# Stick-breaking attention: how densely the preparation of the latent attention is woven in

## The chip, the cores and the metric

The kernel runs on one core of a Trainium2 chip, as one program. The metric is the time of one execution on the device in microseconds (us), as the median of several. The core has five engines with a queue of instructions each: TensorE (PE, matrix products, with its weight loads as PEld), VectorE (DVE), ScalarE (ACT), GpSimd (POOL) and SyncE (SP, which here only starts transfers).

## The reference

Two transformer blocks over 512 tokens of width 1024. The first is a hybrid of pooling and forgetting attention. The second has two attentions side by side, a stick-breaking one and a latent one, and then a sparse feed-forward layer with 16384 experts (PEER). The change concerns the two attentions of the second block:

```python
h = rms_norm(x, attn_norm[l])
proj = h @ w_in[l]
sb_q, sb_k, sb_v, cq, ckv, k_pe = jnp.split(proj, IN_SPLITS, axis=-1)
sb = stick_breaking_attention(sb_q, sb_k, sb_v)          # 8 heads of 64
q = (rms_norm(cq, cq_norm[l]) @ w_uq[l])                 # 384 -> 8 heads of 96
kv = (rms_norm(ckv, ckv_norm[l]) @ w_ukv[l])             # 256 -> 8 heads of 64 + 64
...
q = rms_norm(q, q_norm[l]); k = rms_norm(k, k_norm[l])   # per head
# the last 32 of each head's 96 are rotated by position (rope)
mla = chunk_causal_softmax_attention(q, k, v)
x = x + concat(rms_norm(sb), rms_norm(mla)) @ w_o[l]
x = x + peer_ffn(rms_norm(x, ffn_norm[l]), ...)

# stick-breaking, by blocks of 128 queries, keys s < t:
z = q @ k.T * scale
log_fail = log_sigmoid(-z)
later = cumsum(log_fail, reverse=True) - log_fail
a = exp(log_sigmoid(z) + later); out = a @ v
```

## The kernel before

The program runs through the first block, the second block's attentions and the feed-forward layer one after the other. Products of weights with activations are made of three products of fp32r halves (`mm3`, lines 150 to 152: high by high, low by high, high by low); each weight is streamed in, and split into a high half by ScalarE (line 129) and a low half by a subtraction on the engine in `lo_eng` (line 130), which is DVE, and POOL during the first part of the preparation.

The stick-breaking attention (`sb_attention`) works in 24 steps of one or two pairs of head and query block. A step has at most 512 score columns: for each pair of heads there are two steps with blocks 0 and 2 (128 + 384 columns), two with block 1 (256) and two with block 3 (512). Over its life a step has scores and mask on TensorE (lines 1062, 1063), absolute value, exponential and logarithm on ScalarE, a maximum (line 1074), the running sum as a scan (line 1083) and a subtraction (line 1084) on DVE, a last exponential on ScalarE (line 1094), transposes on TensorE (line 1037), a copy of them by DVE or ScalarE in turn (line 1039) and the products with v (line 1044). The steps are overlapped in 27 rounds; each round gives up control three times, and such a place is a slot.

In these slots other work is drawn, a piece at a time, from a generator `fill2`. Its pieces are in this order: 12 halves of projection tiles for the queries and keys of the stick-breaking attention (`heads_qk`), and 64 pieces that prepare the latent attention (`prep`, line 854): 8 for the query latents, 4 transposes of them (line 197), 8 for the key latents, 4 transposes; then the query up-projection, norm, rotation and transposes of heads by tiles of 128 tokens, and the same for the keys. A query tile's norm is a chain over engines: squares on ScalarE (line 904), their sum and a scaling on DVE (lines 912, 165), a power on POOL (line 166), a multiplication on DVE (line 915), the rotation in six operations on POOL (lines 843 to 850), transposes on TensorE (line 955) and a copy (line 957). For a key tile the lines are 931, 940, 165, 166, 944 and 945, 955, 957; its products are copied at line 932. Key latents are normalised at line 883, also with a power of POOL. PSUM has two banks `mm` for the tiles of all these pieces.

The draw is by a rate: each slot adds the rate to a sum, and each full 1 draws a piece. When the stick-breaking attention has ended, the latent attention (`ml_attention`) starts; its first scores need piece 65, and what is still missing is drawn at once, one piece after the other. Its slots draw one piece each. What orders the instructions in the end is a scheduler that works when the kernel is built: it takes the pieces in the order of the program and may move an instruction ahead where it expects an engine to wait.

The two lines around the rates, and the loop that uses them:

```python
due += 1.0 if "row" in mixed else RATE2 if "sb_done" in mixed else RATE1
while due >= 1.0:
    next(fill)
    due -= 1.0
```

Of the kernel before, what the change touches and what calls it, by code (L numbers as in the profile page):

```python
# [60 lines left out]
def hybrid_mla_peer_kernel(ctx: ExitStack, tc: tile.TileContext, x, meta, gains, rows, bforget, wf, w1v, w1u, poolw,  # L61
# [680 lines left out]
    with ExitStack() as c2:  # L742
# [58 lines left out]

        ready = {0}
        mready = set()
        RATE1, RATE2 = 0.65, 1.0

        def heads_qk():

# [1045 lines left out]
```

## Time and profile before

| | |
|---|---|
| median of three runs | 2052.3 us (2051.57 to 2060.87) |
| profiled execution | 2054.51 us |
| its span, first to last instruction | 2052.6 us, 27008 instructions |
| TensorE busy | 1960.8 us (96%) |
| weight loads busy | 1675.8 us (82%) |
| DVE busy | 1372.1 us (67%) |
| ScalarE busy | 768.5 us (37%) |
| POOL busy | 531.9 us (26%) |
| mean granted clock of TensorE | 0.982 |

The busy time of an engine is the time in which it had an instruction under way; TensorE's ends are modelled, so a busy TensorE is not one at its peak. The shares are means over stages with different limits: the feed-forward layer fills the second half of the span, and the stage of the change lies between 478 and 720 us. In the views below a group or a row has the line, the engine, the operation, and the tiles as out<-in; "idle before <-releaser" is the time that the engine stood before it, and what it then waited for.

### The profile page before, as it was taken

How to read it: one execution, taken by the hardware profiler on the slowest of the kernel's cores; microseconds unless marked ns; L12 is line 12 of the kernel's file. 1: busy time of each engine (PE TensorE's matmuls, PEld its weight loads, DVE VectorE, ACT ScalarE, POOL GpSimd, SP SyncE). 2: the span in 40 equal slices, each digit the busy share in tenths (PEclk: the TensorE clock that was granted, in tenths of full speed). 3: DMA queues.
4: the chain of work that ended last, by engine and by line, in shares of the span. 5: the costliest groups of instructions: out<-in, count | busy, mean ns of one | idle time of the engine just before them, and what ended most of it. 6: DMA issues, size and time to landing. Idle time of an engine off the chain costs nothing.

```text
span 2052.6 us, 27008 instructions
## 1 busy us (share of the span) xinstructions
PE 1960.8 (96%) x10297; PEld 1675.8 (82%) x10297; DVE 1372.1 (67%) x2574; ACT 768.5 (37%) x1228; POOL 531.9 (26%) x476
## 2 busy tenths in 40 slices
PE   7999999999998989998899999999999999999999
PEld 5777688877876778988889788888888888888887
DVE  4324423564577559998997677777777777777785
ACT  4323323254665332223554333333333333333332
POOL 1001100100165026654000133333333333333331
PEclk9999999999999999999999999999999999999999
DMA  4211132422112042213888788888988888888885
GB/s 161 82 62 42 42 102 84 137 77 72 47 42 78 27 154 100 86 52 128 250 244 279 262 295 307 307 282 300 309 292 307 286 297 311 288 308 291 305 279 179
DMA packets 138129, 387.63 MB, mean 189 GB/s; under 512 B 10624, under 2 KB 59904, under 8 KB 129808
## 3 DMA queue, kind: packets, MB, share of 16 engines
q1 hardware_dynamic: 48576, 216.65, 29.6%
q0 software_dynamic: 36864, 134.23, 19.9%
q10 hardware_dynamic: 52560, 35.03, 5.8%
q8 instruction: 80, 1.31, 0.3%
q14 instruction: 49, 0.40, 0.1%
HBM read 357.04 MB, written 28.84 MB: 188 GB/s over the span
## 4 chain that ended last, share of the span: by engine, by line
PE 62%; DVE 16%; issue 8%; DMA 7%; POOL 3%; ACT 3%; ACTq 0%; DVEq 0%; SPq 0%; POOLq 0%
PE mm L152 9%; PE mm L150 9%; PE mm L151 9%; DMA gat<-in_peer_u,idx 4%; PE s L151 3%; PE s L152 3%; PE s L150 3%; PE pt L151 3%; PE pt L152 3%; PE pt L150 3%; DMA gat<-in_peer_v,idx 3%; POOL gat L1616 2%; PE av L1044 1%; PE s L561 1%; PE mi L150 1%
## 5 line engine op out<-in xcount | busy, mean ns | idle before, releaser
L1616 POOL DMA_INDIRECT gat<-in_peer_u,idx x128 | 147.2, 1150 | 466.5 <-DVE acc L1634 233.2
L1616 POOL DMA_INDIRECT gat<-in_peer_v,idx x128 | 147.8, 1154 | 292.7 <-DVE pre L1630 185.3
L1390 DVE TENSOR_TENSOR vlo<-xt,vhi 128x1024 fp32r<-128x1024 f32 x94 | 115.0, 1224 | 126.9 <-ACT vhi L1389 126.1
L152 PE MATMUL mm<-h_hi,ulo 128*128 128x384 f32 x568 | 192.2, 338 | 8.0 <-DVE ulo L1390 8.0
L1389 ACT ACTIVATE vhi<-xt 128x1024 fp32r<-128x1024 f32 x94 | 99.6, 1060 | 262.9 <-PE mi L152 213.0
L150 PE MATMUL mm<-h_hi,uhi 128*128 128x384 f32 x568 | 193.5, 341 | 1.8 <-ACT uhi L1389 1.8
L151 PE MATMUL mm<-h_lo,uhi 128*128 128x384 f32 x568 | 191.3, 337 | 0.0
L130 DVE TENSOR_TENSOR wlo<-wraw,whi 128x2048 fp32r<-128x2048 f32 (+1 forms) x42 | 96.1, 2289 | 136.1 <-ACT whi L129 136.0
L1634 DVE SCALAR_TENSOR_TENSOR acc<-gat,pre,acc 128x1024 f32<-128x1024 f32 x128 | 164.0, 1281 | 33.5 <-DMA gat<-in_peer_v,idx 33.2
L1630 DVE CUSTOM_DVE_ANT_0 gat<-gat,xt 128x1024 f32<-128x1024 f32 x128 | 155.9, 1220 | 42.1 <-DMA gat<-in_peer_u,idx 42.0
L152 PE MATMUL mm<-h_hi,h_lo 128*128 128x384 f32 x456 | 157.3, 345 | 14.8 <-DVE h_lo L1390 10.8
L150 PE MATMUL mm<-h_hi 128*128 128x384 f32 x456 | 157.8, 346 | 10.3 <-ACT h_hi L1389 10.3
L151 PE MATMUL mm<-h_lo,h_hi 128*128 128x384 f32 x456 | 155.9, 342 | 0.0
L129 ACT ACTIVATE whi<-wraw 128x2048 fp32r<-128x2048 f32 (+2 forms) x53 | 97.5, 1840 | 111.0 <-PE mm L151 59.0
L152 PEld LDWEIGHTS mm<-h_hi,ulo 128*128 128x128 f32 x568 | 107.3, 189 | 10.2 <-DVE ulo L1390 10.2
L150 PEld LDWEIGHTS mm<-h_hi,uhi 128*128 128x128 f32 x568 | 107.8, 190 | 4.5 <-ACT uhi L1389 2.7
L151 PEld LDWEIGHTS mm<-h_lo,uhi 128*128 128x128 f32 x568 | 107.6, 189 | 1.8
L150 PE MATMUL mm<-hT_hi,whi 128*128 128x512 f32 x256 | 104.7, 409 | 1.3 <-DVE fz L417 1.0
L150 PE MATMUL s<-vhi,w_hi 128*128 128x512 f32 x256 | 100.3, 392 | 5.0 <-ACT w_hi L1710 5.0
L152 PEld LDWEIGHTS mm<-h_hi,h_lo 128*128 128x128 f32 x456 | 88.0, 193 | 19.4 <-DVE h_lo L1390 14.5
L151 PE MATMUL mm<-hT_lo,whi 128*128 128x512 f32 x256 | 102.1, 399 | 0.0
L152 PE MATMUL mm<-hT_hi,wlo 128*128 128x512 f32 x256 | 102.1, 399 | 0.0
(578 smaller groups left out, 5072.6 us busy)
## 6 DMA issues: line engine op xcount, KB each, us to landing
xt<-in_uT SPq DMA_DIRECT2D x98, 512.0 KB
xt<-in_peer_v SPq DMA_DIRECT2D x94, 512.0 KB
Gd<-stage ACTq DMA_DIRECT2D x24, 1024.0 KB
gate<-Gd SPq DMA_DIRECT2D x16, 1536.0 KB
raw<-in_peer_v SPq DMA_DIRECT2D x34, 512.0 KB
wraw<-in_w1u SPq DMA_DIRECT2D x16, 1024.0 KB
raw<-in_uT SPq DMA_DIRECT2D x30, 512.0 KB
wraw<-in_wpq SPq DMA_DIRECT2D x8, 1024.0 KB
```

What stands on the lines that cost most here:

```text
L129: S.activation(hi[:, :n], r[:, :n], AF.Copy)
L130: lo_eng["e"].tensor_tensor(lo[:, :n], r[:, :n], hi[:, :n].bitcast(F32), op=OP.subtract)
L150: PE.matmul(o, L[0], R[0], start=start, stop=False)
L151: PE.matmul(o, L[0], R[1], start=False, stop=False)
L152: PE.matmul(o, L[1], R[0], start=False, stop=stop)
L561: PE.matmul(s[:, :w], qT[pr, h // 2, tok(qt)], kT[pr, h // 2, n0:16 + n], start=True, stop=False)
L1044: PE.matmul(av[:, col(h, qt):col(h, qt) + 64], pts[i][:, c + j * 128:c + (j + 1) * 128], src[:, j, h * 64:(h + 1) * 64], start=(j == 0), s ...
L1389: S.activation(hi, src, AF.Copy)
L1390: eng.tensor_tensor(lo, src, hi.bitcast(F32), op=OP.subtract)
L1616: G.indirect_dma_start(out=t, out_offset=None, in_=peer_u if kind == "u" else peer_v, in_offset=bass.IndirectOffsetOnAxis(ap=idx[:, s:s + ...
L1630: V.tensor_tensor_reduce(t, t, xt0, 1.0, 0.0, op0=OP.mult, op1=OP.add, accum_out=pre[:, s:s + 1])
L1634: V.scalar_tensor_tensor(acc, t, pre[:, s:s + 1], acc, op0=OP.mult, op1=OP.add)
```

## The change

A single number: the rate at which the slots of the stick-breaking attention draw from `fill2` goes from 0.65 to 0.85 pieces a slot. The rate of the latent attention's slots stays at 1.0.

```diff
@@ -801,7 +801,7 @@
         ready = {0}
         mready = set()
-        RATE1, RATE2 = 0.65, 1.0
+        RATE1, RATE2 = 0.85, 1.0
 
         def heads_qk():
```

What that moves in the order of instructions is seen at three places.

**Place 1**, TensorE, the end of the first half. From the second half of the last tile of key latents (`h_hi`, 288 columns) on; `L197` transposes normalised key latents, `L1062` and `L1063` are scores and mask of a stick-breaking step, `L1037` its transposes, `L1044` its product with v. Before:

```order
L152 MATMUL mm<-whi,h_lo 128x288
L1044 MATMUL av<-sv,pts 128x64 x4
L197 MATMUL mm<-ident,ckn 128x128 x2
L1062 MATMUL s<-sk,sq 128x128
L1063 LDWEIGHTS identb
L1063 MATMUL s<-mask_s,identb 128x128
L1062 MATMUL s<-sk,sq 128x384
L1063 LDWEIGHTS identb
L1063 MATMUL s<-mask_s,identb 128x128
L1037 MATMUL pt<-ident,sbf 128x128 x2
L1044 MATMUL av<-sv,pts 128x64 x2
L1062 MATMUL s<-sk,sq 128x128
```

and now:

```order
L152 MATMUL mm<-whi,h_lo 128x288
L1044 MATMUL av<-sv,pts 128x64 x2
L197 MATMUL mm<-ident,ckn 128x128 x2
L1062 MATMUL mi<-sk,sq 128x256
L1063 LDWEIGHTS identb
L1063 MATMUL mi<-mask_s,identb 128x128
L1037 MATMUL pt<-ident,sbf 128x128 x4
L1044 MATMUL av<-sv,pts 128x64 x4
L1062 MATMUL s<-sk,sq 128x256
L1063 LDWEIGHTS identb
L1063 MATMUL s<-mask_s,identb 128x128
L1037 MATMUL pt<-ident,sbf 128x128
```

Right behind the last product of the tile stood a product with v of full size (`x4`), and now one of half size (`x2`). Behind the first transposes of latents stood a score step of 128 + 384 columns, two transposes and a half product; now two score steps of 256 columns stand there, with four transposes and a full product between them.

**Place 2**, DVE, around the third query tile. `L912` sums the squares, `L165` scales the sum for POOL, `L915` multiplies with POOL's power, `L957` copies transposed query heads, `L130` subtracts a weight half, `L1083` and `L1084` belong to stick-breaking steps. Before:

```order
L912 TENSOR_REDUCE ss_4421<-sqq 128x8
L1084 TENSOR_TENSOR sbf<-mi,sbf 128x512
L165 TENSOR_SCALAR rs_t<-ss_4421 128x8
L915 TENSOR_TENSOR qn<-qn,rs_r 128x768
L1039 COPY pts<-pt 128x512
L130 TENSOR_TENSOR wlo<-wraw,whi 128x2048
L912 TENSOR_REDUCE ss_4492<-sqq 128x8
L957 COPY mqn<-mm 96x4x128
L165 TENSOR_SCALAR rs_t<-ss_4492 128x8
L1101 COPY so<-av 128x4x128
L915 TENSOR_TENSOR qn<-qn,rs_r 128x768
```

and now:

```order
L912 TENSOR_REDUCE ss_4303<-sqq 128x8
L1083 SCALAR_TENSOR_TENSOR sbf<-sbm,sbe 128x128
L165 TENSOR_SCALAR rs_t<-ss_4303 128x8
L1083 SCALAR_TENSOR_TENSOR sbf<-sbm,sbe 128x384
L1039 COPY pts<-pt 128x512
L915 TENSOR_TENSOR qn<-qn,rs_r 128x768
L1074 TENSOR_SCALAR sbm<-s 128x512
L1084 TENSOR_TENSOR sbf<-s,sbf 128x512
L1083 SCALAR_TENSOR_TENSOR sbf<-sbm,sbe 128x128
L1083 SCALAR_TENSOR_TENSOR sbf<-sbm,sbe 128x384
L1084 TENSOR_TENSOR sbf<-s,sbf 128x512
L130 TENSOR_TENSOR wlo<-wraw,whi 128x2048
```

Between `L165` and `L915` of this tile stood nothing; now a scan and a copy stand there, and more scans come between that multiplication and the next weight half.

**Place 3**, TensorE, where the key pieces begin. `L955` transposes query heads, `ck` marks products with the key up-projection. Before:

```order
L1037 MATMUL pt<-ident,sbf 128x128 x4
L955 MATMUL mm<-ident,qn 96x128 x4
L1044 MATMUL av<-sv,pts 128x64 x4
L955 MATMUL mm<-ident,qn 96x128 x4
L1044 MATMUL av<-sv,pts 128x64 x4
L955 MATMUL mm<-ident,qn 96x128 x8
L150 MATMUL mm<-whi,ck_3178 128x512
L151 MATMUL mm<-wlo,ck_3178 128x512
L152 MATMUL mm<-whi,ck_3178 128x512
L150 MATMUL mm<-whi,ck_3178 128x512
L151 MATMUL mm<-wlo,ck_3178 128x512
```

and now:

```order
L1037 MATMUL pt<-ident,sbf 128x128 x4
L1044 MATMUL av<-sv,pts 128x64 x4
L955 MATMUL mm<-ident,qn 96x128 x4
L1062 MATMUL s<-sk,sq 128x512
L1063 LDWEIGHTS identb
L1063 MATMUL s<-mask_s,identb 128x128
L955 MATMUL mm<-ident,qn 96x128 x4
L1037 MATMUL pt<-ident,sbf 128x128 x4
L150 MATMUL mm<-whi,ck_3178 128x512
L151 MATMUL mm<-wlo,ck_3178 128x512
L152 MATMUL mm<-whi,ck_3178 128x512
L150 MATMUL mm<-whi,ck_3178 128x512
```

Before, the last products of the stick-breaking attention stand ahead of the first product with the key up-projection, and none behind it. Now a score step of 512 columns stands ahead of it, and another one, with its transposes and products, comes behind.

## Rows read from the trace of the kernel before

**Rows 1.** Stretches: us, busy PE, PEld, DVE, ACT, POOL, clock, DMA share, GB/s.
```profile
478.30:500.00 21.70, 21.70 (x92) 14.91 (x92) 13.71 (x18) 14.25 (x23) 0.00 (x0) 1.00 0.16 50
...
560.00:580.00 20.00, 20.00 (x145) 17.59 (x144) 13.12 (x29) 12.91 (x36) 6.84 (x22) 1.00 0.00 1
580.00:588.20 8.20, 7.45 (x48) 5.11 (x47) 5.98 (x11) 5.63 (x13) 5.42 (x9) 1.00 0.70 250
588.20:621.50 33.30, 28.71 (x180) 25.56 (x179) 26.05 (x39) 24.07 (x49) 26.52 (x30) 0.95 0.07 28
621.50:654.40 32.90, 26.27 (x147) 20.44 (x148) 19.77 (x42) 13.90 (x49) 23.33 (x26) 0.95 0.21 71
654.40:720.70 66.30, 66.30 (x412) 53.28 (x411) 39.88 (x63) 30.13 (x69) 2.74 (x5) 1.00 0.12 44
```

**Rows 2.** Waits of TensorE, 585 to 655 us: total us, number, longest.
```profile
PE mm L955 <- POOL qn L850: 3.7, 2, 2.9
```

**Rows 3.** Waits of DVE in the same time.
```profile
DVE qn L915 <- POOL rs_r L166: 6.6, 4, 2.0
DVE qn L944 <- POOL rs_r L166: 6.4, 4, 1.8
```

**Rows 4.** Groups of POOL's instructions from 588.2 to 654.4 us.
```profile
L166 POOL TENSOR_TENSOR rs_r<-rs_t,mhalf 128x8 f32<-128x8 f32 x8 | 13.2, 1646 | 7.4 <-DVE rs_t L165 7.3
```

**Rows 5.** The same columns around two gaps.
```profile
606.00:610.00 4.00, 1.07 (x9) 0.93 (x9) 3.90 (x6) 2.00 (x5) 3.03 (x6) 1.00 0.00 0
610.00:614.00 4.00, 4.00 (x17) 3.90 (x18) 2.24 (x4) 1.88 (x4) 3.73 (x5) 0.58 0.00 0
...
628.40:631.00 2.60, 2.60 (x9) 2.17 (x10) 1.00 (x3) 0.00 (x0) 1.68 (x3) 0.50 0.64 271
```

**Rows 6.** TensorE in order of time: start, duration, instruction.
```profile
562.33 0.60 PE L1037 MATMUL pt<-ident,sbf 128*128 128x128 f32 x4
562.77 1.00 PE L1044 MATMUL av<-sv,pts 128*128 128x64 f32 x8
563.58 0.38 PE L150 MATMUL mm<-whi,h_hi 128*128 128x288 f32 x1
...
576.39 1.12 PE L1062 MATMUL mi<-sk,sq 64*128 64x512 f32 x2
...
580.49 0.48 PE L1062 MATMUL s<-sk,sq 64*128 64x128 f32 x2
...
581.06 0.91 PE L1062 MATMUL s<-sk,sq 64*128 64x384 f32 x2
```

**Rows 7.** All engines in order of time, 579 to 586 us.
```profile
579.20 0.29 PE L152 MATMUL mm<-whi,h_lo 128*128 128x288 f32 x1
...
581.08 3.13 POOL L130 TENSOR_TENSOR wlo<-wraw,whi 128x1152 fp32r<-128x1152 f32 x1 [0.38 <-ACT whi L129]
...
585.29 0.44 PE L197 MATMUL mm<-ident,ckn 128*128 128x128 f32 x2 [0.75 <-DVE ckn L883]
```

**Rows 8.** Groups of DVE's instructions from 478 to 660 us, shapes apart.
```profile
L1083 DVE TENSOR_TENSOR_SCAN sbf<-sbm,sbe 128x512 f32<-128x512 f32 x8 | 10.9, 1363 | 5.4 <-PE pt L1037 2.0 <-ACT junkb L171 1.7 <-ACT sbe L1088 1.6
...
L1074 DVE TENSOR_SCALAR sbm<-s 128x512 f32<-128x512 f32 x12 | 8.2, 687 | 19.8 <-ACT sbe L1073 19.8
...
L1084 DVE TENSOR_TENSOR sbf<-s,sbf 128x512 f32<-128x512 f32 x12 | 8.2, 681 | 0.2
```

**Rows 9.** POOL and DVE in order of time, 608 to 627 us.
```profile
608.22 1.38 POOL L848 TENSOR_TENSOR rb<-qn,cs 128x128 f32<-128x128 f32 x1
...
615.45 2.59 DVE L130 TENSOR_TENSOR wlo<-wraw,whi 128x2048 fp32r<-128x2048 f32 x1 [0.68 <-ACT whi L129]
...
615.86 2.50 POOL L847 TENSOR_TENSOR ra<-qn,cs 128x128 f32<-128x128 f32 x1
...
618.32 0.45 POOL L848 TENSOR_TENSOR rb<-qn,cs 128x128 f32<-128x128 f32 x1
...
623.24 3.03 POOL L843 TENSOR_TENSOR ra<-qn,cs 128x128 f32<-128x128 f32 x1 [1.07 <-DVE qn L915]
```

## The prediction

> **What bounds the kernel now.** I read the page first: TensorE is busy 96% of the span, so a change in the order of one stage is worth only what TensorE stands still, or runs slowly, in that stage. The stage here lasts from 478.3 us (first scores of the stick-breaking attention) to 654.4 us (last transposes of the latent keys); I next asked for each engine's busy time by stretches of it [rows 1]. The reader is to see two halves. From 478.3 to 580, five stretches, TensorE is busy all the time while VectorE (DVE) works 13.71 of 21.70 us in the first and 13.12 of 20.00 in the last: TensorE is the limit. From 588.2 on that ends: TensorE works 28.71 of 33.30 and 26.27 of 32.90 us, and GpSimd (POOL), nearly idle before, 26.52 and 23.33. After 654.4 TensorE is full again. With the 0.75 us missing at 580 to 588.2 it stands 4.59 + 6.63 + 0.75 = 12.0 us.
>
> Whom it waits for there stands in the list of waits: first of all, up to 2.9 us at a time, for a rotary product of POOL before query heads can be transposed [rows 2]. The waits of DVE in the same time say more: eight times a multiplication (L915, L944) stands for the power that POOL takes of the sum of squares, 6.6 + 6.4 = 13.0 us [rows 3]; the power itself has 1646 ns each [rows 4]. What is queued behind such a multiplication on DVE, scans of the stick-breaking attention and copies of transposed weights, stands too, although it needs nothing from POOL, and TensorE waits for those copies. Last I read the clock around the long gaps [rows 5]: after TensorE was busy 1.07 of 4.00 us, the granted clock is 0.58 in the next 4 us; another stretch of 2.6 us has 0.50, the lower level, 1.2 of 2.4 GHz. In time that is 0.42 x 4.0 + 0.50 x 2.6 = 3.0 us. All that the stage could give back is 12.0 + 3.0 = 15.0 us, 0.73% of the span.
>
> **What the change does, and its cost.** No instruction is added or removed. The stick-breaking attention has 24 steps in 27 rounds of three slots, 81 slots; at 0.65 it draws 52 pieces of the filling work, at 0.85 it draws 68 of the 76. The 37th piece, the first product with the query up-projection, comes after 44 slots instead of 57. In the order of TensorE's instructions 7 of the 24 score steps now follow that product, where 3 did: four steps leave the half in which TensorE is the limit and enter the half in which it waits. From the first scores of the latent attention on, the order is almost the same on every engine, and the transposes of the last keys stand at nearly the same place; so the whole effect lies before 654.4 us, and what follows moves with it.
>
> Term 1, the first half, up to that product (588.2 us before). The four steps that leave it are one with a single head of 512 columns, two with 128 + 384, one with 256. Their price by TensorE's rows [rows 6]: scores of 512 columns 1.12 us, of 128 + 384 0.48 + 0.91 = 1.4; four transposes 0.44 (from 562.33 to 562.77), eight rows of a product with v 0.81 (562.77 to 563.58). That is 2.4 and 2.65 us a step; the 256-column step is taken at somewhat over half, 1.3. So 2.4 + 2 x 2.65 + 1.3 = 9.0, and as TensorE is full there, the half gets 9 us shorter.
>
> Term 2, a wait at the end of that half. The transposes of key latents at 585.29 waited 0.75 us for the normalised tile of DVE (L883), which waited for a power that POOL could only take after it had subtracted two weight halves, the second at 581.08 for 3.13 us [rows 7]. From the last product of that tile (579.20 + 0.13, its distance to the next) to 585.29 this took 6.0 us, of which other work of TensorE covered 5.2. In the new order less stands there: a product with v of half size (0.4), the first transposes of latents (0.3, some two of the four), scores of 256 columns twice (0.7 each), transposes (0.44 + 0.1) and a product with v (0.8), 3.4 us. And between the two halves of the tile stand only transposes (0.44), where scores of 512 columns and two transposes stood (1.3); TensorE gets there 0.9 us earlier against POOL's subtractions. The wait becomes 6.0 + 0.9 - 3.4 = 3.5 us, 2.7 more than before. Its bounds are -0.75, if nothing is left of it, and some 3.2, if a scan stretches a subtraction by another 0.5.
>
> Term 3, the second half, 66.2 us before. Here DVE decides, as I read it: its busy time of 26.05 + 19.77 = 45.8 [rows 1] and its 13.0 of standing for POOL make 58.8 of the 66.2; the other 7.4 are waits for TensorE and ScalarE. Four more steps bring DVE four maxima, scans, subtractions and, in every second step, a copy: by its means [rows 8] 0.69 + 1.36 + 0.68 and half of another 0.68, 3.1 us for each of the three large steps; 1.8 as an estimate for the small one. Of these 11 us I take 10, since neighbours on DVE overlap by some 0.08. The waits for POOL's power: a bare one, with nothing between the sum (L165) and the multiplication, is 1.8 (the four of L944 come to 6.4, the longest of each kind are 1.8 and 2.0). In the new order three are bare; in the others a scan of 384 columns and a copy (1.6 together), a maximum and a copy (0.9), or one instruction of 0.3, 0.6 and 0.6 stand between. That is 3 x 1.8 + 0.2 + 0.9 + 1.5 + 1.2 + 1.2 = 10.4 instead of 13.0. Of the other 7.4 most should go, since TensorE and ScalarE have steps to hand over while DVE stands; I take 2. The half then lasts 45.8 + 10 + 10.4 + 2 = 68.2, 2.0 longer.
>
> Sum: -9 + 2.7 + 2.0 = -4.3 us. TensorE's own work in the second half would be 54.98 - 3.0 + 9 = 61 us; it no longer sets this half, and there most of the possible 15 us stays. The bounds: with no wait left anywhere -9 - 0.75 + (61 - 66.2) = -15.0; with DVE's 13.0 and 7.4 all kept, 76.2 us in the second half, -9 + 2.7 + 10 = +3.7. I take the value that follows the order, nearer to the upper end, because DVE's chain with POOL is in the rows, and that it disappears is not.
>
> One rule speaks against the change. While DVE subtracted a weight half of 2048 columns (2.59 us at 615.45), a rotary product of POOL took 2.50, and another 3.03 beside the next such half; its like take 0.45 [rows 9]. The Trainium skill, SBUF - State Buffer, section "Who interferes with whom", states that a DVE instruction with two SBUF inputs contends with a GpSimd instruction that reads SBUF, and that whichever starts first holds the shared ports for the whole instruction. The trace agrees by these rows. Scans read two tiles as well, and 10 scan instructions instead of 4 stand behind the first query norm on DVE; this is rival C.
>
> **Rivals.** A: TensorE is fed throughout; the steps fill every gap, and none is long enough for the clock to fall. For it: of the second half, the part that still had three steps lost TensorE 4.6 us, the part without any 6.6 [rows 1]. Against it: DVE would have 45.8 + 10 us of work in 61 and could stand for POOL only 5 us of 13. From -10.3 to -15 us: about 2040.
>
> B: the four steps cost in the second half what they free in the first. DVE keeps its 13.0 us of standing and 4 of the other 7.4: 45.8 + 10 + 13 + 4 = 72.8, +6.6; -9 + 2.7 + 6.6 = +0.3: 2052.5. For it: the three bare waits, with steps queued behind each. Against it: the five that are covered.
>
> C, slower: scans hold up POOL. Place: the rotary products and powers of the four query tiles. The scan at 607.9 made one rotary product 1.38 long [rows 9], 0.9 more; if all six further scan instructions do so, POOL's chain, which feeds DVE, is 5.4 us longer, and two more gaps of over 3 us follow, each with the lower clock at 1.5 us: 72.8 + 5.4 + 3.0 = 81.2, and -9 + 2.7 + 15.0 = +8.7: 2061. For it: POOL works 49.85 of the 66.2 us already. Against it: only some of the scans can meet a rotary product. It decides once the second half passes 72.5 us.
>
> That the change moves nothing is excluded by the order (7 steps against 3).
>
> **How the numbers follow.** The profiled execution took 2054.5 us, the span and 1.9 around it; that is 2.2 above the median of three, 2052.3. The sum is a difference between stretches of one execution (from whose time it would give 2050.2), so I take it from the median: 2048. Chances: forecast (-1.5 to -10 us) 0.56; A 0.13; B (within 1.5) 0.19; C 0.12, of it 0.05 beyond 10 us. A measurement of this kernel can tell about 0.5%, 10.3 us, from no change. Faster by more than that is A, 0.13; slower by more, the far part of C, 0.05; within, 0.82. The likeliest case's own range is 2042 to 2051; with B and the near parts of A and C, 2041 to 2056 leaves out some 0.15.
>
> **What would show it.** Right: the first up-projection product near 582 us; before it a wait of TensorE of 3 to 4 us for L883; DVE's standing for POOL's power down to 10 or 11 us; stick-breaking work between the key pieces that had none; the last key transposes near 650; and no stretch after that changed in length. Wrong: a second half near 61 us means that DVE was not the limit (A); over 72.5 us, with DVE's standing at 13 or more and longer rotary products, is B or C; if a stretch after the last key transposes changes by over 2 us, the effect isn't closed in this stage, and my premise falls.

## The result, and the profile after

The changed kernel is slower: 2071.83 us as the median of ten runs beside 2058.28 us of the kernel before, ratio 1.0065, 95% interval 1.004 to 1.009. Timed again (run `again` below) the ratio was 1.0091, 1.0061 to 1.012. That is 13.6 us more in these ten runs; the forecast was 4.3 us less, and its range ended at 2056, 3.7 us above the median that it started from.

The first view is that of [rows 1], by the changed kernel's own stretches: the first half up to the first product with the query up-projection, from there to the first product with the key up-projection, from there to the end of the last key transposes, and the rest of the latent attention. The columns are those of [rows 1].

```profile
478.68:582.20 103.52, 101.22 (x546) 80.45 (x545) 53.84 (x90) 55.51 (x112) 19.91 (x36) 0.98 0.17 59
582.20:620.17 37.97, 33.20 (x188) 26.99 (x186) 26.72 (x41) 25.11 (x50) 28.87 (x33) 0.90 0.08 28
620.17:663.00 42.83, 34.83 (x197) 28.57 (x197) 27.73 (x51) 19.26 (x57) 21.93 (x21) 0.86 0.15 50
663.00:732.84 69.84, 68.97 (x417) 54.95 (x416) 40.28 (x67) 32.61 (x77) 3.19 (x6) 0.98 0.12 42
```

The same four stretches took 110.0, 33.3, 33.0 and 66.2 us before. The first half is 6.5 shorter; the two that follow are 4.7 and 9.8 longer, and the last, which was to move unchanged, 3.6. The stage, from the first stick-breaking scores to the end of the latent attention's last product, takes 254.2 us instead of 242.4. The span grew by 18.1; the 6 us that come later than this stage say nothing, since `again`, the same program, had 10 us more there than this profile.

Where did the 11.8 us go? I cut the stage into pieces of 2 us and added up, for each, the time TensorE stood, and its busy time by one less the granted clock. TensorE's work at full clock is what is left, and it is nearly the same: 227.4 us before, 226.3 after. It stood 12.0 us before and 15.9 after; the lower clock cost 3.1 before and 12.0 after. So a third of the loss is standing, and two thirds are time at 1.2 GHz. Five stretches show it, after five gaps of 1.6 to 3.0 us; three of them, with the gap before the first and the third (columns as above, [rows 5] of before):

```profile
575.40:577.60 2.20, 0.00 (x0) 0.00 (x0) 0.51 (x2) 0.36 (x2) 2.20 (x6) 0.92 0.83 350
577.60:582.00 4.40, 4.37 (x13) 2.75 (x14) 2.62 (x6) 1.38 (x4) 0.55 (x4) 0.50 0.70 281
...
618.00:622.00 4.00, 4.00 (x15) 3.05 (x15) 3.97 (x6) 1.44 (x3) 2.93 (x5) 0.55 0.18 74
634.00:636.80 2.80, 0.00 (x0) 0.00 (x0) 2.80 (x5) 0.31 (x1) 0.80 (x1) 0.73 0.00 0
636.80:642.00 5.20, 5.15 (x18) 4.24 (x19) 3.44 (x8) 1.60 (x5) 3.05 (x3) 0.50 0.01 2
```

What TensorE and DVE waited for, 565 to 665 us (us in total, number, longest; [rows 2, 3] of before):

```profile
PE mm L150 <- DVE so L932: 5.2, 2, 2.9
PE mm L955 <- POOL qn L850: 3.0, 1, 3.0
PE mm L955 <- POOL qn L945: 2.3, 2, 1.6
PE mm L197 <- DVE ckn L883: 2.3, 1, 2.3
```

```profile
DVE qn L915 <- POOL rs_r L166: 8.3, 4, 2.6
DVE qn L944 <- POOL rs_r L166: 5.5, 4, 1.8
DVE so L932 <- ACT sqq L931: 5.0, 4, 3.2
...
DVE mkn L957 <- PE mm L955: 3.8, 2, 3.2
```

Two things go against the forecast. DVE stands 13.8 us for POOL's power, not 10.4 as I had it (13.0 before). And at the head of TensorE's list is a wait that before did not have at all: key products wait for L932, a copy of the value half of an earlier key product, because that copy keeps one of the two `mm` banks. All engines around the first of these two waits, in order of time:

```profile
632.04 0.69 DVE L944 TENSOR_TENSOR qn<-qn,rs_r 128x512 f32<-128x512 f32 x1 [1.71 <-POOL rs_r L166]
...
632.64 3.23 DVE L1083 TENSOR_TENSOR_SCAN sbf<-sbm,sbe 128x512 f32<-128x512 f32 x2
632.81 0.39 ACT L931 ACTIVATE sqq<-mm 128x256 f32<-128x256 f32 x1
...
635.80 0.66 DVE L1084 TENSOR_TENSOR sbf<-s,sbf 128x512 f32<-128x512 f32 x1
636.38 0.41 DVE L932 COPY so<-mm 128x256 f32<-128x256 f32 x1
...
636.85 0.80 PE L150 MATMUL mm<-whi,ck 128*128 128x512 f32 x1 [2.95 <-DVE so L932]
```

The copy could have run at 633.2, when ACT was through with the bank. DVE had first stood 1.71 us for a power, and then two scans and a subtraction of late stick-breaking steps stood ahead of it. TensorE lost 2.95 us there, and 2.6 at the lower clock up to 642.

The second wait for L932 is of another kind, with no scan ahead of its copy:

```profile
648.82 0.39 ACT L931 ACTIVATE sqq<-mm 128x256 f32<-128x256 f32 x1
...
651.09 1.20 DVE L944 TENSOR_TENSOR qn<-qn,rs_r 128x512 f32<-128x512 f32 x1 [1.75 <-POOL rs_r L166]
...
652.21 0.41 DVE L932 COPY so<-mm 128x256 f32<-128x256 f32 x1
...
652.76 0.77 PE L150 MATMUL mm<-whi,ck 128*128 128x512 f32 x1 [2.24 <-DVE so L932]
```

ACT was through with that bank at 649.2; what kept the copy back was a power that DVE stood for and the multiplication with it. The same pair, L944 and then L932, stands in DVE's order before as well (645.90 and 647.04 us), and no wait of TensorE for L932 of over 0.6 us came of it there.

### The profile page after: what moved, and what is told of

Read it like the earlier page. It is cut to its first block, busy times and chain, and to the rows that moved or that the text cites. A ratio compares the mean times of both kernels' runs of the same rounds, so it can differ in the third digit from the quotient of the medians.

```text
span 2070.7 us, 27004 instructions
## 1 busy us (share of the span) xinstructions
PE 1972.4 (95%) x10297; PEld 1685.1 (81%) x10297; DVE 1370.4 (66%) x2574; ACT 768.6 (37%) x1228; POOL 533.4 (26%) x476
## 4 chain that ended last, share of the span: by engine, by line
PE 64%; DVE 15%; issue 7%; DMA 6%; POOL 4%; ACT 3%; ACTq 0%; DVEq 0%; SPq 0%; POOLq 0%
PE mm L152 10%; PE mm L150 10%; PE mm L151 9%; PE s L151 3%; PE s L152 3%; PE s L150 3%; PE pt L152 3%; PE pt L151 3%; PE pt L150 3%; DMA gat<-in_peer_u,idx 3%; DMA gat<-in_peer_v,idx 3%; POOL gat L1616 2%; PE mi L150 1%; PE av L1044 1%; PE mi L152 1%
## 5 line engine op out<-in xcount | busy, mean ns | idle before, releaser
L130 DVE TENSOR_TENSOR wlo<-wraw,whi 128x2048 fp32r<-128x2048 f32 (+1 forms) x42 | 95.9, 2284 | 146.1 <-ACT whi L129 146.0
L150 PEld LDWEIGHTS mm<-h_hi 128*128 128x128 f32 x456 | 88.7, 194 | 17.7 <-ACT h_hi L1389 16.3
## 6 DMA issues: line engine op xcount, KB each, us to landing
gate<-Gd SPq DMA_DIRECT2D x16, 1536.0 KB, 10.3
```

Of the source, the lines that this page charges most:

```text
L130: lo_eng["e"].tensor_tensor(lo[:, :n], r[:, :n], hi[:, :n].bitcast(F32), op=OP.subtract)
L150: PE.matmul(o, L[0], R[0], start=start, stop=False)
```

## The experiments

The theories: **K**, the lower clock behind the gaps is most of the loss; **D**, scans of late steps ahead of the value copies in DVE's queue make the gaps (by the rows above, the first of the two waits for L932; the second has no scan); **Q**, the chains with POOL's power set the second half, and each step moved there lengthens it; **P**, rival C of the prediction, POOL held up by the shared port. The stage, TensorE's standing and the loss at the lower clock are read from one profile each, as above. "End" is when the latent attention's last product ends; in four kernels (`vact065`, `ln65`, `lnlovact`, `all65`) the scheduler put the first scores 1 to 2.6 us earlier, so that there the end compares better than the stage. Where the last column is empty, the kernel was executed once only.

| run | rate, edit | stage | stood | clock | end | time, ratio to before |
|---|---|---|---|---|---|---|
| before | 0.65 | 242.4 | 12.0 | 3.1 | 720.7 | |
| after | 0.85 | 254.2 | 15.9 | 12.0 | 732.8 | 1.0065 (1.004 to 1.009) |
| again | 0.85 | 254.3 | 15.9 | 12.3 | 733.0 | 1.0091 (1.0061 to 1.012) |
| vact | 0.85, value copies on ACT | 244.6 | 10.9 | 6.7 | 723.0 | |
| vact5 | the same | 244.6 | 10.9 | 6.7 | 723.4 | 0.9997 (0.9977 to 1.0017) |
| two | 0.85, then 0.60 | 245.0 | 11.4 | 6.6 | 723.4 | 1.0006 (0.9985 to 1.0027) |
| lnexp | 0.85, power on ACT | 237.7 | 7.3 | 3.1 | 716.3 | |
| lnexp5 | the same | 239.1 | 7.4 | 4.7 | 717.3 | 0.9974 (0.9956 to 0.9993) |
| port | 0.85, subtractions in pieces | 251.3 | 13.5 | 10.7 | 730.5 | |
| lov | 0.85, two subtractions to DVE | 250.7 | 12.8 | 11.3 | 729.5 | |
| warmck | 0.85, products in a gap | 251.4 | 16.0 | 6.6 | 730.2 | |
| warmqn | 0.85, products in a gap | 252.0 | 11.1 | 11.6 | 730.7 | |
| r075 | 0.75 | 238.2 | 9.5 | 1.6 | 717.0 | 0.9984 (0.9966 to 1.0003) |
| r100 | 1.0 | 254.2 | 15.4 | 12.8 | 732.9 | 1.0065 (1.0037 to 1.0092) |
| vact065 | 0.65, value copies on ACT | 243.2 | 11.4 | 4.8 | 718.9 | 0.9983 (0.9964 to 1.0002) |
| ln65 | 0.65, power on ACT | 239.7 | 6.7 | 6.0 | 715.4 | 0.9971 (0.9944 to 0.9999) |
| ln75 | 0.75, power on ACT | 241.0 | 7.3 | 7.3 | 719.7 | 0.9968 (0.9934 to 1.0001) |
| lnlovact | 0.85, all three edits | 232.8 | 6.1 | 0.0 | 709.7 | 0.9918 (0.9891 to 0.9946) |
| all65 | 0.65, all three | 243.8 | 10.8 | 5.4 | 721.1 | 1.0036 (1.0009 to 1.0063) |
| all100 | 1.0, all three | 239.4 | 7.8 | 6.7 | 718.3 | 0.9963 (0.9931 to 0.9994) |

**The spread** (`again`, no edit).

> The changed kernel once more, unchanged, for the spread between executions. The stage, from the first stick-breaking scores to the end of the last product of the latent attention, took 242.4 us before and 254.2 after. All theories: 254 within 1 again, with the same waits of TensorE (2.3 for the key latents, 3.0 for a rotary product, 2.9 and 2.2 for the copies of L932). If the stage differs by over 3 us, single profiles can't be set against each other. What comes after the stage may differ by some 6 us, as it did between the two profiles so far.

The stage repeats within 0.1 us, with the same waits: the order is fixed, and so are the gaps. The clock repeats in sum (12.0 and 12.3), but not stretch by stretch, as told at the end.

**The value copies** (`vact`, `vact5`).

```diff
-                V.tensor_copy(mv[:, tt, n * 256:(n + 1) * 256]...
+                S.copy(mv[:, tt, n * 256:(n + 1) * 256]...
```

> Rate 0.85; the copy of the value half of a key product (L932) goes from DVE to ACT, so that it no longer stands behind scans of late stick-breaking steps in DVE's queue. Theory D (scans ahead of the copies keep the PSUM banks, and TensorE waits): the waits of 2.9 and 2.2 us go, and the lower clock behind them (2.4 + 1.2 us); the stage takes 246 to 248. Theory P (scans hold up POOL by the shared port, rival C of the prediction): the waits there were for DVE by name only, the stage stays at 253 to 255. Theory K alone gives the same as D, as these gaps are two of its five.

> Rate 0.85 with the copy of the value half on ACT, now timed; one profile gave a stage of 244.6 us. Theory D: 0.1% above the time of the kernel before (2.2 us) with an interval that holds 1.0, and below the changed kernel, which was 0.65 and 0.91% above. If the gain of that profile was the clock alone, 0.5% above before.

The waits for L932 fall from 5.2 to 0.2 us, the stage from 254.2 to 244.6, in both profiles: 5.0 less standing, 5.3 less at the lower clock. With this copy of 0.4 us, eight times, on another queue most of the loss is gone, and the time is that of the kernel before. DVE still stands 14.7 us for the power here (8.3 and 6.4), so these 9.6 us were not the price of the standing by itself, but of what is behind it in the queue.

**The place of the late steps** (`two`). As many steps follow the first up-projection product as at 0.85, but none the first key product (`LATE` is 0.60, and "uq" is set with the first piece of the query up-projection).

```diff
-            due += 1.0 if "row" in mixed else RATE2 if "sb_done" in mixed else RATE1
+            due += 1.0 if "row" in mixed else RATE2 if "sb_done" in mixed else LATE if "uq" in mixed else RATE1
```

> Rate 0.85 until the query up-projection begins, 0.60 from there, so that as many steps follow the first up-projection product as in the changed kernel (6.0 of 512 columns), but none of them the first product with the key up-projection (1.0 there). Theory D (scans in front of the copies of L932 between key pieces): the two waits for L932 are gone, the stretch from the first key product to the last key transposes takes 33 to 35 us instead of 42.0, the stage 244 to 247 instead of 254.2. Theory Q (each step that is moved to the second half lengthens the chains there, wherever it stands): the stretch before the key pieces grows by what the one behind it loses, the stage takes 251 to 255. Time: D 2.5% of nothing, that is 2058 to 2062 beside 2056 of the kernel before; Q 2068.

(The "2.5% of nothing" in it is a slip; the range behind it is what was expected.) 245.0 is D's number, by another way than `vact`: the copies stay on DVE, and no score step follows the first key product. Of its scans two still come behind that product on DVE (621.6 and 626.0 us), one of them right ahead of the first value copy, but none between a standing for the power and a copy; TensorE's waits for these copies are 0.6. Q, by which the place should not matter, falls in that form.

**The power** (`lnexp`, `lnexp5`): POOL's instruction of 1.65 us becomes a logarithm and an exponential on ACT.

```diff
-        G.tensor_tensor(r[:p, :cols], t[:p, :cols], mhalf[:p, :cols], op=OP.pow)
+        if cols == 8:
+            S.activation(t[:p, :cols], t[:p, :cols], AF.Ln)
+            S.activation(r[:p, :cols], t[:p, :cols], AF.Exp, scale=-0.5)
+        else: ...
```

> Rate 0.85; the power of the norms of the query and key heads (128x8) goes from POOL (one instruction of 1.65 us) to ACT (a logarithm and an exponential). Theory Q: what DVE stands for POOL's power, 8.3 + 5.5 us, falls to some 4, and the stage by half of that or more, to 246 to 249. Theory D: the standing falls as well, but the waits for L932 stay, since scans stand ahead of the copies as before; ACT has more to do in front of the squares; stage 251 to 254.

> Rate 0.85 with the power of the head norms on ACT, now timed; one profile gave a stage of 237.7 us (242.4 before, 254.2 at 0.85). Theory Q: 0.2% or more below the time of the kernel before (4.7 of 2056), and 0.6 to 0.9% below the changed kernel. If the profile was a lucky one (the lower clock behind the same gaps cost 1.5 to 4.6 us in different profiles), the stage comes out at 240 to 243 now and the time at that of before.

This gave more than either theory had expected. DVE's standing, 565 to 665 us, in `lnexp5` (`rs_r` now comes from ACT, and L919 and L948 are the two multiplications):

```profile
DVE qn L919 <- ACT rs_r L168: 1.0, 1, 1.0
...
DVE qn L948 <- ACT rs_r L168: 0.4, 1, 0.4
```

13.8 us became 1.4. Scans still stand ahead of the value copies, and yet TensorE's waits for these fall from 5.2 to 2.0: a queue that is not late forgives an order that is bad. So D and Q are two halves of one thing, and either half taken away takes most of the loss. DVE takes its instructions in order; it is late by the powers it stands for, then, at the first of the two waits, the scans come, and the copy behind is what TensorE needs.

**The port** (`port`), each subtraction of 2048 columns in four.

```diff
+            for c in range(0, n, lo_w["n"]):
+                sl = slice(c, min(n, c + lo_w["n"]))
-            lo_eng["e"].tensor_tensor(lo[:, :n], r[:, :n], hi[:, :n].bitcast(F32), op=OP.subtract)
+                lo_eng["e"].tensor_tensor(lo[:, sl], r[:, sl], hi[:, sl].bitcast(F32), op=OP.subtract)
```

> Rate 0.85; the two subtractions of weight halves that run on DVE in the second half of the preparation (2048 columns, 2.3 us each) are cut into four of 512. Theory P in its narrow form (the subtraction held one rotary product, L849, for 2.50 us instead of 0.58, and TensorE waited 3.02 us for that query tile): the rotary product takes at most 1.0, the wait falls to 1 to 1.5 us, the clock of 0.60 and 0.55 at 614 to 622 stays at 1.00, the stage takes 249 to 251. Theory D: that gap is as long as before or goes to another place, and the two later ones stay; the stage takes 253 to 254.

The rows of the held rotary product and of the subtraction beside it, in the changed kernel, and of the same product here (three lines further down in this kernel):

```profile
612.25 2.30 DVE L130 TENSOR_TENSOR wlo<-wraw,whi 128x2048 fp32r<-128x2048 f32 x1
612.37 2.50 POOL L849 TENSOR_TENSOR qn<-ra,rb 128x128 f32<-128x128 f32 x1
...
614.20 0.90 POOL L852 TENSOR_TENSOR qn<-ra,rb 128x128 f32<-128x128 f32 x1
```

From 2.50 to 0.90, and the wait of 3.0 falls to 1.9: the hold is real. The clock fell to 0.59 and 0.50 there all the same, and 2.9 us is all the stage gained. Nor is that the price of the port alone: a piece of a subtraction came between the scans in DVE's queue, and the first wait for L932 (2.95) went with it. The port explains one gap of five, and before had one like it, of 2.92.

**The key latents' wait** (`lov`) and the clock behind it.

```diff
+            lo_eng["e"] = V
             for tt in range(TT):
                 yield from ck_tile(us, tt)
```

> Rate 0.85; the two subtractions of weight halves (1152 columns, some 3.1 us each on POOL) that stood ahead of POOL's power for the last key latents go to DVE. Theory K: the wait of 2.3 us for the key latents (L883) goes, and with it the lower clock behind it (3.2 us in one profile, 1.7 in the other); the first up-projection product comes 4 to 5.5 us earlier, the stage takes 249 to 250.5. If the prediction's term 2 was right in counting the wait alone, the product comes 2.3 us earlier and the stage takes 252.

The wait goes (2.3 to 0.2), so term 2 had its cause right. The first up-projection product comes 1.9 us earlier, not 4 to 5.5: in this profile the clock fell once near the start of the stage, where TensorE had no gap at all, and that cost 1.7 us.

**Is it the gap that lowers the clock?** (`warmck`, `warmqn`): products that nothing uses, ahead of the transposes that wait.

```diff
+        def warm(b, n):
+            for _ in range(n):
+                PE.matmul(b, identb, mask_s.unsqueeze(1).to_broadcast([128, 4, 128]), start=True, stop=True)
```

> Rate 0.85; ahead of the third transposes of key latents ten products of 512 columns in bf16 are put on TensorE, written to the bank that the transposes fill afterwards. They fill the gap of 2.27 us there; the rest of the order is almost the same. Theory K (8.6 of the 12 us are TensorE's lower clock behind such gaps): the clock stays 1.00 where it fell to 0.50 at 577.6 to 582 and 0.74 to 586, the first up-projection product comes 2.5 to 3 us earlier (at 579.5 instead of 582.2), the stage takes about 251. Theory Q (the chains over DVE, ACT and POOL set the time, the clock only follows): the product may come earlier, but the chains behind it take it back, the stage stays at 253 to 254. If the clock falls although TensorE was busy, K is wrong about its cause.

> Rate 0.85; thirteen products of 512 columns in bf16 ahead of the transposes of the third query tile, written to the bank that these fill afterwards; TensorE waits 3.0 us there for a rotary product, and the bank should be free by then. Theory K: TensorE stays busy, the clock stays 1.00 at 614 to 622 (lost there: 3.15 us), and the stretch from the first up-projection product to the first key product takes 35 us instead of 38.0. Theory Q: the clock stays up and the stretch takes 37 to 38 all the same, since DVE and POOL set it. If the clock falls although the products ran in the gap, K is wrong about its cause.

`warmck` missed its aim: the products waited 2.28 us themselves, so the wait of [rows 7] is for the bank and not for the data: what these transposes read had been made at 569.05, and the bank was not free, since L883 still had to read the last tile in it. Its stage is 2.8 us shorter all the same, with the same standing (16.0), by the clock alone (6.6 instead of 12.0, with 2.5 us of the added products against it); that is no more than the spread told at the end. `warmqn` met its aim. Its stretches: the filled gap, what follows, the next gap, and what follows that:

```profile
612.30:615.30 3.00, 2.99 (x15) 1.20 (x14) 3.00 (x3) 2.75 (x6) 3.00 (x3) 1.00 0.00 0
615.30:618.30 3.00, 2.73 (x15) 1.55 (x15) 2.16 (x6) 1.63 (x3) 2.77 (x3) 1.00 0.85 265
618.30:620.40 2.10, 0.00 (x0) 0.00 (x0) 2.10 (x4) 0.61 (x2) 1.15 (x3) 0.86 0.31 125
620.40:624.40 4.00, 3.98 (x13) 3.42 (x13) 4.00 (x6) 1.74 (x6) 2.78 (x5) 0.50 0.00 0
```

With the gap filled the clock stays at 1.00, where it was 0.60 and 0.55. But TensorE then ran ahead into the next wait (2.2 us, for a copy of query heads on DVE), and the clock fell there, for 6.5 us in all. The stretch to the first key product took 39.3, no less than 38.0. At this gap K has the cause of the clock right, in one profile; as a cure it does nothing as long as the chains behind are late. (That the clock also falls without a gap is told at the end.)

**More and less of it** (`r075`, `r100`), the constant alone.

> The rate at 0.75: 4.0 steps of 512 columns behind the first up-projection product (2.5 before, 6.0 at 0.85), none behind the first key product. Theory D: no wait for L932; the stage takes 240 to 245 (242.4 before), the time is that of before. Theory Q: by the steps moved, 1.5 of 3.5, it takes 247. Both hold if half of the loss is the lower clock behind the wait for the key latents (L883): then that wait decides, 2.3 us at 0.85, and it should be 1 to 1.5 here.

> The rate at 1.0: 7.5 steps of 512 columns behind the first up-projection product and 3.0 behind the first key product (6.0 and 1.0 at 0.85), eight scans behind the first value copy. Theories D and Q both: longer than at 0.85, D more so: the stretch from the first key product to the last key transposes 50 us or more (42.0), the stage 260 to 265, time 1% or more above before. If the loss at 0.85 came from the wait for the key latents and its clock alone, 254 to 257, as that wait grows by 1 at most.

At 0.75 the stage is 4.2 us shorter than before, what the prediction gave 0.85, though the interval of the time still holds 1: no score step behind the first key product, 0.4 us instead of 2.3 for the key latents, 1.6 lost at the lower clock. At 1.0 both theories were wrong: 254.2, no longer than at 0.85, with 1.7 us of waits for L932. (The number is that of the third case in the expectation, but not by its reason: the wait for the key latents is 1.0 there.) In their place stands one of 5.0 us for another copy on DVE, of transposed query heads, with 4.6 us at the lower clock behind it. About as much was lost in the first half: TensorE waited 2.2 us for the query latents (L868), and 6.8 went to the lower clock behind that. The rows of DVE around the wait of 5.0:

```profile
598.13 1.75 DVE L915 TENSOR_TENSOR qn<-qn,rs_r 128x768 f32<-128x768 f32 x1 [4.18 <-POOL rs_r L166]
599.79 0.68 DVE L1039 COPY pts<-pt 128x512 f32<-128x512 f32 x1
...
602.76 0.68 DVE L957 COPY mqn<-mm 96x512 f32<-96x512 f32 x1
```

It is the same figure with another copy in it: a power DVE stands for, stick-breaking work, and behind both what frees a bank. Which copy it hits is the order's accident, and the loss does not grow in step with the rate.

**Controls for the edits** (`vact065`, `ln65`, `ln75`).

> The kernel before (0.65) with the copy L932 on ACT: the control for the gain of 9.6 us that this edit brought at 0.85. Theory D: no scan stands ahead of that copy at 0.65, so there is nothing to win: stage 241 to 243, time within 0.2%. If the copy on ACT is simply better (DVE is the limit in the key pieces by its busy time), the stage gains 3 us or more here too.

> The kernel before (0.65) with the power of the head norms on ACT, as in the run at 0.85 that took 237.7 us for the stage. Theory Q (DVE standing for POOL's power is the limit of the second half in both kernels): the stage takes 234 to 238 instead of 242.4, time 0.2 to 0.4% less than before; and the order of the rates turns: 0.85 is no longer slower than 0.65. If the standing mattered only together with the late steps, the stage takes 240 to 242.

> Rate 0.75 with the power of the head norms on ACT. No long wait for the key latents (0.4 at 0.75, 2.3 at 0.85) and no scan ahead of the value copies: all theories 232 to 236 for the stage, time 0.4 to 0.6% less than before. If ACT is now too full between the squares and the exponentials of the stick-breaking steps, 238.

At 0.65 the value copy on ACT leaves the stage within 1 us (243.2), and the time within 0.2%: that edit is worth something only where the copies come late enough for TensorE to wait. The power on ACT ends the stage 5.3 us earlier at 0.65 and 16 us earlier at 0.85; with 239.7 `ln65` came out between the two ranges expected. `ln75` (241.0) missed the 232 to 236 expected, with 5.6 lost in one stretch at the lower clock. By time the three rates are alike once the power is on ACT (0.9971, 0.9968 and 0.9974): the order of the rates did not turn, the denser weaving just costs nothing any more.

**All three edits** (`lnlovact`, `all65`, `all100`).

> Rate 0.85 with all three causes taken away: the head norms' power on ACT, the value copies on ACT, the two subtractions of weight halves in front of the key latents' power on DVE instead of POOL. If they add up, the stage loses the 2.3 us wait with its low clock (3.2) beside what the power gave: 231 to 234, time 0.4 to 0.6% below before. If ACT is too full now (its copies of 0.4 us stand between squares and exponentials) or DVE is (2.6 us more in the first half), 236 to 239, no better than the power alone.

> The three edits (head norms' power and value copies on ACT, the two subtractions on DVE) at the old rate 0.65. If 0.85 lost only by those three waits and the clock behind them, the denser weaving is worth what the prediction's rival A said once they are gone: the stage at 0.65 takes 237 to 240, 4 us or more above the 232.8 at 0.85, the time 0.2 to 0.5% below before (0.82% at 0.85). If the gain is that of the edits alone, whatever the rate, 231 to 235 here too.

> The three edits at rate 1.0. If the denser weaving keeps paying once the three waits are gone: stage 229 to 232, time 0.9% or more below before. If new waits take their place where eight scans stand among the key pieces (a copy of query heads waited 5.0 us for DVE at 1.0 without the edits): 236 to 242, time 0.4 to 0.6% below.

The kernel with the three edits at 0.85 beats both, by 0.82% (0.54 to 1.09) to the kernel before. Its second half, the two stretches as above:

```profile
576.88:607.99 31.11, 30.22 (x189) 25.42 (x189) 28.20 (x42) 24.69 (x56) 22.76 (x26) 1.00 0.11 40
607.99:640.91 32.92, 30.14 (x196) 24.93 (x196) 25.52 (x44) 21.50 (x74) 14.33 (x19) 1.00 0.15 51
```

TensorE's clock is 1.00 throughout and it stands 3.7 us: with the waits gone the steps nearly fill the half, as rival A had it. The control missed its range of 237 to 240: the same edits at 0.65 gain nothing (243.8; TensorE waits 7.3 us for rotary products there), and its time, 0.36% above before, is more than its stage explains; that stays open. It is also not the best kernel at 0.65: `ln65`, with the power alone, ends its stage at 715.4, 5.7 us behind `lnlovact`, and that is the clock, which cost 6.0 there and nothing here (standing 6.7 and 6.1). At 1.0 the stage is 239.4: its second half loses nothing to the clock, but its first half 6.7, behind a wait of 2.2 us for the query latents that the less dense kernels do not have.

## Why the prediction was wrong, point by point

**What bounds the stage** held: TensorE in the first half, DVE and its chain with POOL behind.

**Terms 1 and 2** held in sum: 6.5 us off the first half, 6.3 forecast. In the parts errors met: the wait for the key latents was 2.3 and not 3.5, but the lower clock that followed it cost 2.3 before the first up-projection product, which I had not charged, though [rows 5] showed that a gap is paid twice. Term 1 by itself was then nearer to -10.3 than -9. So that the sum came out is luck. And the wait that I read in [rows 7] as one for the normalised tile is one for the bank, by `warmck`.

**Term 3 failed.** The second half took 80.8 us, not 68.2. In its own terms: DVE's busy time 54.4 (55.8 forecast) was right; the standing for POOL 13.8 (10.4); and "of the other 7.4 most should go, since TensorE and ScalarE have steps to hand over while DVE stands; I take 2" became 12.6. This is the step that failed. It took DVE's work and its standing as a sum, and asked only whether DVE had something to do. It did not ask what stands behind the scans in DVE's queue and who waits for that: the value copies, which free banks (`vact`, -9.6; `two`, -9.2). And the standing that I counted as unavoidable is what makes the queue late in the first place (`lnexp` and `lnexp5`, -16.5 and -15). The upper bound of +3.7 fell for the same reason: it kept the other waits at the 7.4 of before and had no place for new ones.

**The clock** was the second omission. The term took TensorE's work there as 61 us at full clock; it was busy 68.0, of which 8.2 were lost at the lower clock. Gaps of 2.2 us and more were one before [rows 2] and four after; in the rivals I charged for the clock, in the forecast not.

**The closed stage** failed as well: what follows the last key transposes is 3.6 us longer, over the 2 us that I had named as the sign. Some 1.5 of it is the clock after the last gap, 0.9 standing.

**Rival B** had the standing (13.0, and it is 13.8) but kept 4 of the other waits, where 12.6 came.

**Rival C** had the size (81.2 for the second half) and the wrong mechanism: POOL's busy time there is 50.8 us, 49.85 before, so it grew by 1 and not by 5.4. Scans did hold it (three rotary products beside the scans at 620.4 took 0.84 to 0.88 us, their like 0.45), but hardly delayed it. The rule on the shared port that the prediction cited (the Trainium skill, SBUF - State Buffer, "Who interferes with whom") is borne out by `port` for one gap, and that one was there before. Its part on who starts first is not: of the two pairs in [rows 9] the product of 3.03 us started first, at 623.24, the subtraction at 623.68 (2.28 us long), and by the profile it was the product that was held. Rival C had named gaps with the clock behind them, and those came, from DVE's queue.

**Rival A** had in mind what `lnlovact` shows: with the three waits gone the second half has 3.7 us of standing and a clock of 1.00. That the denser weaving itself pays is not shown. `lnlovact` ends 11 us ahead of `all65`, but only 5.7 ahead of `ln65`, no more than the clock took from that one profile.

## What to carry to other kernels

Where work moves into a half that an in-order engine limits, don't add up that engine's work; list what stands behind each moved instruction in its queue, and ask of each whether it frees a bank or a buffer that the busiest engine needs. Such copies belong on the queue that nothing long shares. Charge new gaps of TensorE for the clock as well: here five of them, 12.0 us together, cost about as much again; and when a change of order loses, look for the wait it made before giving up the order: here removing the waits, by three edits, turned +0.65% into -0.82%.

## What the runs showed of the hardware

The price of a gap at the lower clock is not fixed. Behind the same wait of 2.28 us for the key latents it was 3.2 us in the profile of after, 1.7 in `again`, 3.4 in `vact` and 4.8 in `lnexp5`. Nor does it need a long gap: in `ln65` the clock fell after a wait of 0.75 us that cost nothing in the kernel before, and in `lov`, `again` and `ln75` near 482 us after score products alone, without any wait (`lov`, columns as in [rows 1]):

```profile
480.00:481.80 1.80, 1.80 (x8) 0.80 (x8) 0.69 (x1) 1.23 (x2) 0.00 (x0) 1.00 0.00 0
481.80:484.00 2.20, 2.20 (x8) 1.72 (x8) 1.32 (x3) 1.92 (x4) 0.00 (x0) 0.54 0.00 0
```

That the number of slow products differs between runs of one kernel is also what the Trainium skill says (TensorE: Matmul & The Clock Gate, section "Part 1: The HAM clock gate"), there of those at a kernel's start; `after` and `again` agree, with 3.2 and 1.7 us behind the same wait. What else decides the runs don't show; with prices from 1.7 to 4.8 us behind one wait, two stages closer than some 3 us can't be told apart by one profile each.
